# Reordering the blocks of a state-space scan, preparing a table's parts inside the loop before, and joining two matmuls of a feed-forward into a wide one

## The chip, the cores and the metric

The kernel runs on one core of a Trainium2 chip. The metric is the device time of one execution in microseconds (us). Five engines work side by side, each through its own instructions in order: TensorE (PE, with its weight loads as PEld), VectorE (DVE), ScalarE (ACT), GpSimd (POOL) and SyncE (SP), which issues the DMAs from HBM. The profile names them by these short forms.

## What is computed

Two model blocks over 256 tokens of width 1024, all in float32. The parts that the change touches are these, cut from the reference:

```python
# block 1: complex-diagonal state-space scan (32 groups of 16 channels, 64 states)
bu_re = jnp.einsum('blgc,gpc->blgp', uf, bbar_re)
bu_im = jnp.einsum('blgc,gpc->blgp', uf, bbar_im)
_, _, h_re, h_im = lax.associative_scan(_complex_scan_combine, (a_re, a_im, bu_re, bu_im), axis=1)
y = (jnp.einsum('blgp,gcp->blgc', h_re, c_re) - jnp.einsum('blgp,gcp->blgc', h_im, c_im)
     + d_skip * uf)
...
# block 1, end: retrieval of single-neuron experts, 16384 rows in each table
a = jnp.einsum('cd,ced->ce', xb, u_tab[eb])
w = gb * jax.nn.gelu(a, approximate=False)
out = jnp.einsum('ce,ced->cd', w, v_tab[eb])
...
# block 2, two layers, after the attention of each
h = _rms_norm(x, mlp_norm[l])
x = x + jnp.square(jax.nn.relu(h @ w_ff1[l])) @ w_ff2[l]     # 1024 -> 4096 -> 1024
```

Around them stand a window attention with its gates and branches in block 1, and compressed, selected and latent attention in block 2.

## The kernel before

The program is written in a tile framework. The code gives every instruction a priority that mostly follows the order in which it is written; at build time the framework fixes each engine's order from these priorities and the dependences. On the chip each engine goes through that order and waits at an instruction whose operands are not there yet.

**Weights.** A `Stream` loads weight pieces of 128 x 1024 float32 (512 KB) in one order through 3 raw buffers. For most products it splits a piece into a high part `whi` (cast by ACT, L120) and a remainder `wlo` (subtraction on DVE or POOL, L122), in two halves of 512 columns, through 3 buffers each. A product is then three matmuls: high times high, high times low, low times high.

**The scan.** `s5_scan` runs eight blocks of two groups each, in the background of other products: a generator whose steps are taken two at a time between the weight pieces of the query/key/value projection (L238, 24 matmuls of 512 columns on unsplit weights) and of the gates (L218, 128 of 256 columns). A block first makes a cosine and a sine table on DVE and POOL (L673 to L678) and its inputs by four matmuls (L683) into PSUM tiles `sc`; then rotates the inputs by the tables on DVE (L692 to L696), scans along the first 128 tokens (L703), carries over (L709 to L714), scans the second 128 (L717), rotates back (L720 to L723), and multiplies by the output matrix on PE (L730, eight matmuls). Each of these is one step, block after block. PE's order is thus projection matmuls with the scan's own matmuls among them. The attention scores of block 1 (L842, and L847 on DVE) use the same two banks `sc` as L683.

**The expert tables.** `peer` goes through the first table in 128 pieces. The step of a piece is 24 matmuls of 256 columns (L205 to L207); the activations (L986, L987, L989) land in `store`, one column of tokens per piece. Once the retrieval's choices are decoded, `quad` multiplies `store` by the routing weights, four tokens at a time, 64 times, spread over the pieces up to number `LAST` = 126 (L971, L972 on PE, L976 on DVE, L978 on ACT). Then the pool of that part is closed and the pool `pv` opened; `split` makes the parts `wh` and `wl` of a column of `store` (L1016 on ACT, L1017 on DVE), two columns ahead, and `gemm_acc` multiplies them with the second table's 128 pieces, 12 matmuls of 512 columns each (L273 to L275).

**The feed-forward.** `mlp` takes the first matrix in 32 pieces by `gemm_t`: for each of 8 contraction steps, three matmuls of 256 columns into one PSUM tile (L205 to L207). `evict` takes relu and the row scale on DVE (L1548), the square on ACT (L1549), the high part on ACT (L1550) and the remainder on DVE (L1551). The low parts of the weights alternate between DVE and POOL (`F1`). Three PSUM banks rotate. The second matrix follows with `gemm_acc` (12 matmuls of 512 columns per piece, 32 pieces).

Of the kernel before, what the change touches and what calls it, by code (L numbers as in the profile page):

```python
# [7 lines left out]
F32 = mybir.dt.float32  # L8
# [17 lines left out]
LAST = 126  # L26
# [170 lines left out]

class Kernel:
# [94 lines left out]
    def tokens(self):  # L293

        return [self.stay.tile([128, 8, T], F32R, name=n, tag=n) for n in ("xh", "xl")]

# [29 lines left out]
    def transposed_parts(self, src, i, xh, xl, tp, rev=None):  # L326

        n = src.shape[-1] // 128
        for k0 in range(0, n, 4):
# [9 lines left out]
            self.split_t(ps[:, :m], xh[:, k0:k0 + m, ts], xl and xl[:, k0:k0 + m, ts])  # L339
# [319 lines left out]
    def s5_scan(self, w, p, uT):  # L659
# [5 lines left out]
        for x in range(8):  # L665
            t, j0, n0 = x // 2, 2 * (x % 2), 2 * (x % 4)
            js = slice(2 * x, 2 * x + 2)
# [16 lines left out]
            yield  # L684
            tabs = [x.rearrange("p j a b -> p j (a b)") for x in (tc, ts)]
            cb, sb = [x.unsqueeze(2).to_broadcast([128, 2, 2, 128]) for x in tabs]
# [8 lines left out]
            yield  # L695
# [9 lines left out]
            yield  # L705
# [13 lines left out]
            yield  # L719
# [4 lines left out]
            yield  # L724
            if j0 == 0:
                yps = self.tp.tile([128, T], F32, name="tp", tag="tp")
            for i, (c, z) in enumerate(((self.cre, q2), (self.cre, q1), (self.cim, q3), (self.cn, im))):
                for j in range(2):
                    r = 32 * (j0 + j)
                    te.matmul(yps[r:r + 32].rearrange("p (u t) -> p u t", u=2), c[:, 2 * x + j], z[:, j],  # L730
                              start=i == 0, stop=i == 3)
            if j0:
                v.scalar_tensor_tensor(uT[:, t], uT[:, t], dsk[:, t:t + 1], yps, op0=OP.mult, op1=OP.add)
            yield
# [160 lines left out]
    def peer(self):  # L895
# [4 lines left out]
        with ExitStack() as outer:  # L900
# [4 lines left out]
            off = [0]  # L905

# [12 lines left out]
            with ExitStack() as ctx:  # L919
# [72 lines left out]
                def step():  # L992
# [7 lines left out]
                    while done["q"] < min(want, T // 4):  # L1000
                        quad(done["q"])

                self.gemm_t(128, 8, xh, xl, evict, step=step)
                while done["q"] < T // 4:
                    quad(done["q"])

            with ExitStack() as ctx:
                w = ctx.enter_context(tc.tile_pool(name="pv", bufs=1))
                ps = self.acc4(5, 6, 7, 3)
                self.next_gain("attn_norm_0")  # L1010
                parts = {}

                def split(c):
                    wh = w.tile([128, T], F32R, name="wh", tag="wh", bufs=3)
                    wl = w.tile([128, T], F32R, name="wl", tag="wl", bufs=3)
                    s.copy(wh, store[:, c])  # L1016
                    v.tensor_tensor(out=wl, in0=store[:, c], in1=wh.bitcast(F32), op=OP.subtract)  # L1017
                    parts[c] = wh, wl
# [692 lines left out]
```

## Time and profile before

| | us |
|---|---|
| median of 3 runs (1743.00 to 1745.09) | 1744.74 |
| the profiled execution | 1741.02 |
| its span, first to last instruction | 1739.2 |
| scan, under the query/key/value projection (40 to 110) | 70.0 |
| scan and attention, under the gates (110 to 200) | 90.0 |
| second expert table, from 732.4 on | 349.6 |
| first feed-forward matrix, layer 0 and layer 1 | 93.1, 93.2 |

The span is where the argument is made; the remainder of the profiled execution, 1.8 us, lies around it. A matmul's record lasts longer than the distance to the next start, since matmuls are pipelined; the pace is read from starts. A row of the timeline names the engine, line, operation and tiles; in square brackets stands how long the engine was idle before it and which instruction ended that. float32 matmuls on unsplit operands (L218, L238, L683, L730) have two records each.

### The profile page before, as it was taken

What the parts mean: (1) busy time and instruction counts of PE and PEld (TensorE: products, weight loads), DVE (VectorE), ACT (ScalarE), POOL (GpSimd) and SP (SyncE); (2) the same over time, 40 slices, a digit from 0 to 9 for tenths busy, and PEclk for the clock granted to TensorE, in tenths of its full rate; (3) what the DMA queues carried; (4) which work ended last, traced back from release to release, by engine and by line L of the source; (5) the groups of instructions that cost most, each with busy time, mean ns of one, the idle gap of its engine ahead of it and who ended that gap; (6) DMA issues with size and microseconds to landing.
All of it is one profiled execution on the core that took longest, in us unless ns stands there. A gap on an engine that the chain in (4) does not pass through costs nothing.

```text
span 1739.2 us, 30119 instructions
## 1 busy us (share of the span) xinstructions
PE 1679.5 (97%) x10796; PEld 1467.5 (84%) x10796; DVE 1066.5 (61%) x2590; ACT 871.6 (50%) x2054; POOL 600.0 (34%) x502
## 2 busy tenths in 40 slices
PE   7989998999999999999999999899999999999998
PEld 4467987999999999988888887787998878789986
DVE  5877344469878888755555555677653256775422
ACT  2014444454555554455555555655665455656643
POOL 1210365555000000044444444412544443144443
PEclk9999998899999999999999999999999999999999
DMA  6332445454655555556566665533555653335554
GB/s 224 109 96 73 135 144 160 135 187 138 183 160 158 162 161 164 170 177 193 193 193 193 193 194 183 173 103 122 172 189 187 194 180 123 134 132 189 181 192 143
DMA packets 81537, 282.34 MB, mean 162 GB/s; under 512 B 9659, under 2 KB 12524, under 8 KB 81388
## 3 DMA queue, kind: packets, MB, share of 16 engines
q1 hardware_dynamic: 81388, 280.43, 50.5%
q8 instruction: 85, 1.39, 0.3%
q14 instruction: 64, 0.52, 0.1%
HBM read 279.32 MB, written 1.07 MB: 161 GB/s over the span
## 4 chain that ended last, share of the span: by engine, by line
PE 82%; DVE 8%; POOL 4%; ACT 2%; issue 2%; DMA 2%; SPq 0%; POOLq 0%; DVEq 0%; ACTq 0%
PE acc L205 11%; PE acc L206 11%; PE acc L207 11%; PE acc L275 10%; PE acc L273 10%; PE acc L274 10%; PE acc L218 3%; POOL wlo L122 2%; PE o L1427 2%; PE acc L243 1%; PE acc L242 1%; PE acc L241 1%; ACT whi L120 1%; PE sc L1390 1%; PE g L971 1%
## 5 line engine op out<-in xcount | busy, mean ns | idle before, releaser
L122 POOL TENSOR_TENSOR wlo<-raw,whi 128x512 fp32r<-128x512 f32 (+2 forms) x396 | 518.8, 1323 | 947.8 <-ACT whi L120 903.6
L120 ACT CAST whi<-raw 128x512 fp32r<-128x512 f32 (+2 forms) x940 | 545.0, 613 | 402.1 <-PE acc L206 173.2
L122 DVE TENSOR_TENSOR wlo<-raw,whi 128x512 fp32r<-128x512 f32 (+2 forms) x544 | 412.0, 772 | 268.2 <-ACT whi L120 257.8
L205 PE MATMUL acc<-xh,whi 128*128 128x256 f32 x1664 | 477.9, 288 | 0.7 <-ACT xh L321 0.7
L207 PE MATMUL acc<-xh,wlo 128*128 128x256 f32 x1664 | 472.6, 284 | 1.6 <-DVE wlo L122 1.6
L206 PE MATMUL acc<-xl,whi 128*128 128x256 f32 x1664 | 472.6, 284 | 0.1
L207 PEld LDWEIGHTS acc<-xh,wlo 128*128 128x128 f32 x1664 | 320.4, 193 | 2.5 <-DVE wlo L122 1.8
L205 PEld LDWEIGHTS acc<-xh,whi 128*128 128x128 f32 x1664 | 320.3, 193 | 2.4 <-ACT xh L321 1.4
L206 PEld LDWEIGHTS acc<-xl,whi 128*128 128x128 f32 x1664 | 320.6, 193 | 1.4 <-issue 0.4
L273 PE MATMUL acc<-whi,wh 128*128 128x512 f32 x512 | 200.0, 391 | 2.8 <-ACT wh L1016 2.8
L274 PE MATMUL acc<-wlo,wh 128*128 128x512 f32 x512 | 199.8, 390 | 0.0
L275 PE MATMUL acc<-whi,wl 128*128 128x512 f32 x512 | 199.5, 390 | 0.0
L1016 ACT CAST wh<-store 128x256 fp32r<-128x256 f32 x128 | 52.0, 408 | 161.1 <-PE acc L274 160.2
L1017 DVE TENSOR_TENSOR wl<-store,wh 128x256 fp32r<-128x256 f32 x128 | 54.2, 425 | 115.3 <-ACT wh L1016 115.3
L273 PEld LDWEIGHTS acc<-whi,wh 128*128 128x128 f32 x512 | 96.5, 189 | 23.1 <-ACT wh L1016 3.0
L274 PEld LDWEIGHTS acc<-wlo,wh 128*128 128x128 f32 x512 | 96.6, 189 | 19.9
L275 PEld LDWEIGHTS acc<-whi,wl 128*128 128x128 f32 x512 | 96.4, 188 | 19.8
L274 PE MATMUL acc<-wlo,fh 128*128 128x512 f32 x256 | 99.7, 389 | 0.0
L275 PE MATMUL acc<-whi,fl 128*128 128x512 f32 x256 | 99.7, 389 | 0.0
L273 PE MATMUL acc<-whi,fh 128*128 128x512 f32 x256 | 99.6, 389 | 0.0
L218 PE MATMUL acc<-xt,raw 128*128 128x256 f32 x320 | 76.8, 389 | 0.0
L218 PEld LDWEIGHTS acc<-xt,raw 128*128 128x128 f32 x320 | 59.6, 193 | 12.5 <-issue 3.9
(384 smaller groups left out, 2443.7 us busy)
## 6 DMA issues: line engine op xcount, KB each, us to landing
raw<-in_peer_u_dram SPq DMA_DIRECT2D x128, 512.0 KB, 3.6
raw<-in_peer_v_dram SPq DMA_DIRECT2D x128, 512.0 KB, 4.3
raw<-in_w_ff_dram SPq DMA_DIRECT2D x128, 512.0 KB, 3.9
raw<-in_w_out_dram SPq DMA_DIRECT2D x24, 512.0 KB, 3.7
raw<-in_w_in_g_dram SPq DMA_DIRECT2D x16, 512.0 KB, 3.6
raw<-in_w_in_qkv_dram SPq DMA_DIRECT2D x12, 512.0 KB, 3.6
raw<-in_w_attn_branch_dram SPq DMA_DIRECT2D x8, 512.0 KB, 3.9
raw<-in_peer_w_query_dram SPq DMA_DIRECT2D x8, 512.0 KB, 3.9
```

Source lines behind the costliest of these rows:

```text
L120: nc.scalar.copy(hi[:, x], src[:, x])
L122: eng.tensor_tensor(out=lo[:, x], in0=src[:, x], in1=hi[:, x].bitcast(F32), op=OP.subtract)
L205: t.matmul(ps, wh, xh, start=first, stop=False)
L206: t.matmul(ps, wh, xl, start=False, stop=False)
L207: t.matmul(ps, wl, xh, start=False, stop=last)
L218: self.nc.tensor.matmul(ps, wh[:, k, m], xh[:, k], start=k == 0, stop=k == kt - 1)
L273: t.matmul(ps[i][n], xh[:, ts], w[0][:, ns], start=first, stop=False)
L274: t.matmul(ps[i][n], xh[:, ts], w[1][:, ns], start=False, stop=False)
L275: t.matmul(ps[i][n], xl[:, ts], w[0][:, ns], start=False, stop=last)
L1016: s.copy(wh, store[:, c])
L1017: v.tensor_tensor(out=wl, in0=store[:, c], in1=wh.bitcast(F32), op=OP.subtract)
L1427: te.matmul(o[:, 4 * b + x], st[u][:, c, x], val, start=c == 0, stop=c == i)
```

## The change

It has three parts. In `s5_scan` the steps become functions, and their order is new: the inputs of block x+1 (its tables and its four matmuls) stand ahead of the back-rotation of block x, and the outputs of block x stand behind the first rotation of block x+1. In `peer`, `LAST` is 124; the buffers of `wh` and `wl` lie in the outer pool; and columns 0 and 1 of `store` are split inside the first table's loop as soon as all 64 quads are done. In `mlp`, the high and low part of the tokens lie side by side in a tile, the matmuls high-high and high-low become one of 512 columns, and `evict` adds the two halves of the result, by a copy on ACT and an addition on DVE.

```diff
-LAST = 126
+LAST = 124
...
+class Halves:
+    def __init__(self, x, n):
+        self.x, self.n = x, n
+    def __getitem__(self, key):
+        p, ks, *ts = key
+        return self.x[ks.start // 4][(p, slice(0, 4), self.n, *ts)]
...
+    def tokens(self, both=False):
+        if both:
+            x = [self.stay.tile([128, 4, 2, T], F32R, name=n, tag=n) for n in ("xh", "xl")]
+            return x, [Halves(x, n) for n in range(2)]
...
+    def gemm_2(self, n_sub, x, evict):
+        t = self.nc.tensor
+        for s in range(n_sub):
+            wh, wl = [z.rearrange("p (k c) -> p k c", c=128) for z in self.S.get()]
+            ps = self.acc.tile([128, 2, T], F32, name="acc", tag="acc")
+            for k in range(8):
+                z = x[k // 4][:, k % 4]
+                if k:
+                    t.matmul(ps[:, 0], wl[:, k], z[:, 0], start=False, stop=False)
+                t.matmul(ps, wh[:, k], z, start=k == 0, stop=k == 7)
+                if k == 0:
+                    t.matmul(ps[:, 0], wl[:, k], z[:, 0], start=False, stop=False)
+            evict(s, ps)
...
-        for x in range(8):
...
+        inputs(0)
+        yield
+        for x in range(9):
+            if x < 8:
+                rotate(x)
+                yield
+            if x:
+                outputs(x - 1)
+                yield
+            if x < 8:
+                for f in (scan_1, scan_2):
+                    f(x)
+                    yield
+                if x < 7:
+                    inputs(x + 1)
+                    yield
+                back(x)
+                yield
...
+            def split(c):
+                wh = pst.tile([128, T], F32R, name="wh", tag="wh", bufs=3)
+                wl = pst.tile([128, T], F32R, name="wl", tag="wl", bufs=3)
...
+                    if done["q"] == T // 4 and c < 128 and 0 not in parts:
+                        split(0)
+                        split(1)
                 self.gemm_t(128, 8, xh, xl, evict, step=step)
-                while done["q"] < T // 4:
-                    quad(done["q"])
...
-                    if c == 0:
-                        split(0)
-                        split(1)
...
-                xh, xl = self.tokens()
+                x, (xh, xl) = self.tokens(True)
...
-                    v.scalar_tensor_tensor(r, ps, 0.0, row, op0=OP.max, op1=OP.mult)
+                    s.copy(r, ps[:, 1])
+                    v.tensor_tensor(out=r, in0=ps[:, 0], in1=r, op=OP.add)
+                    v.scalar_tensor_tensor(r, r, 0.0, row, op0=OP.max, op1=OP.mult)
                     s.activation(q, r, AF.Square)
...
-                self.gemm_t(32, 8, xh, xl, evict)
+                self.gemm_2(32, x, evict)
```

Three places show what this does to the engines' orders. The lines of the kernel after differ: L249 and L229 there are L238 and L218 before, L718 is L683, L783 is L730.

PE under the query/key/value projection, from the inputs of one scan block on (L683, L718: inputs; L730, L783: outputs), before:

```order
L683 MATMUL sc<-uT,bb 128x256 x4
L238 MATMUL acc<-raw,xt 128x512 x9
L730 MATMUL tp<-s5x,s5c 32x256 x6
L730 MATMUL tp<-bu,cn 32x256 x2
L238 MATMUL acc<-raw,xt 128x512 x3
L683 MATMUL sc<-uT,bb 128x256 x4
L238 MATMUL acc<-raw,xt 128x512 x11
```

and after:

```order
L718 MATMUL sc<-uT,bb 128x256 x4
L249 MATMUL acc<-raw,xt 128x512 x8
L718 MATMUL sc<-uT,bb 128x256 x4
L249 MATMUL acc<-raw,xt 128x512 x4
L783 MATMUL tp<-s5x,s5c 32x256 x6
L783 MATMUL tp<-bu,cn 32x256 x2
L249 MATMUL acc<-raw,xt 128x512 x8
L718 MATMUL sc<-uT,bb 128x256 x4
```

The inputs of the second block now stand ahead of the outputs of the first, and twelve projection matmuls lie between one block's outputs and the next block's.

ACT at the end of the first expert table (L986, L1065: activation of a piece; L978, L1057: a quad's copy; L1016, L982: high part of a `store` column), before:

```order
L978 ACTIVATE store<-g 128x2x4
L120 CAST whi<-raw 128x512
L986 ACTIVATE gt<-acc 128x256
L120 CAST whi<-raw 128x512 x2
L986 ACTIVATE gt<-acc 128x256
L120 CAST whi<-raw 128x512
L1016 CAST wh<-store 128x256 x4
```

and after:

```order
L1057 ACTIVATE store<-g 128x4x4
L982 CAST wh<-store 128x256 x3
L120 CAST whi<-raw 128x512
L1065 ACTIVATE gt<-acc 128x256
L120 CAST whi<-raw 128x512 x2
L1065 ACTIVATE gt<-acc 128x256
```

The first three `wh` now stand ahead of the activations of the last four pieces; before, they stood behind the last one.

DVE in the first feed-forward matrix, away from its ends (L1548, L1617: relu and scale; L1551, L1620: remainder of the square; L1616: the new addition), before:

```order
L1548 SCALAR_TENSOR_TENSOR fr<-acc,row 128x256
L122 TENSOR_TENSOR wlo<-raw,whi 128x512 x2
L1551 TENSOR_TENSOR fl<-fq,fh 128x256
L1548 SCALAR_TENSOR_TENSOR fr<-acc,row 128x256
L1551 TENSOR_TENSOR fl<-fq,fh 128x256
```

and after:

```order
L1616 TENSOR_TENSOR fr<-acc,fr 128x256
L1617 SCALAR_TENSOR_TENSOR fr<-fr,row 128x256
L122 TENSOR_TENSOR wlo<-raw,whi 128x512 x2
L1620 TENSOR_TENSOR fl<-fq,fh 128x256
L1616 TENSOR_TENSOR fr<-acc,fr 128x256
L1617 SCALAR_TENSOR_TENSOR fr<-fr,row 128x256
L1620 TENSOR_TENSOR fl<-fq,fh 128x256
```

The order is the old one with the addition put ahead of each scale. ACT's order there, after (L1615 is the new copy, L1618 the square, L1619 its high part):

```order
L120 CAST whi<-raw 128x512 x2
L1618 ACTIVATE fq<-fr 128x256
L1619 CAST fh<-fq 128x256
L1615 COPY fr<-acc 128x256
L120 CAST whi<-raw 128x512 x2
```

The copy of a piece stands behind the high part of the piece before, and the next weights' two casts lie between copy and square.

## Rows read from the trace of the kernel before

**Rows 1.** The page: an engine's busy time; a DMA's size and time to landing.

```profile
PE 1679.5 (97%) x10796; PEld 1467.5 (84%) x10796; DVE 1066.5 (61%) x2590; ACT 871.6 (50%) x2054; POOL 600.0 (34%) x502
...
raw<-in_peer_v_dram SPq DMA_DIRECT2D x128, 512.0 KB, 4.3
```

**Rows 2.** Stretches: length, busy PE, PEld, DVE, ACT, POOL, granted clock, DMA share, GB/s.

```profile
40.00:110.00 70.00, 63.17 (x247) 31.07 (x245) 61.68 (x162) 9.33 (x20) 16.53 (x10) 1.00 0.35 107
110.00:200.00 90.00, 89.56 (x554) 71.29 (x551) 53.75 (x181) 33.86 (x100) 8.23 (x7) 1.00 0.26 84
...
732.00:739.00 7.00, 4.25 (x16) 3.33 (x15) 2.97 (x5) 2.43 (x6) 1.79 (x2) 0.76 0.64 207
...
1229.00:1322.10 93.10, 93.10 (x777) 92.89 (x776) 51.43 (x101) 60.47 (x131) 45.94 (x35) 1.00 0.58 187
```

**Rows 3.** Waits between 30 and 205: us in total, times, longest.

```profile
DVE s5x L692 <- PE sc L683: 13.2, 4, 5.3
...
PE tp L730 <- DVE s5x L720: 6.7, 5, 3.2
```

**Rows 4.** Timeline of PE in the scan: start, us, what, [idle before <-releaser].

```profile
81.90 7.13 PE L238 MATMUL acc<-raw,xt 128*128 128x512 f32 x16
...
108.44 1.49 PE L730 MATMUL tp<-s5x,s5c 128*32 128x256 f32 x12 [3.15 <-DVE s5x L720]
```

**Rows 5.** Timeline of all engines where the second expert table begins.

```profile
730.95 0.42 DVE L987 TENSOR_TENSOR store<-gt,store 128x256 f32<-128x256 f32 x1
...
732.32 0.28 PE L207 MATMUL acc<-xh,wlo 128*128 128x256 f32 x1
...
733.31 1.27 POOL L122 TENSOR_TENSOR wlo<-raw,whi 128x512 fp32r<-128x512 f32 x1 [0.79 <-ACT whi L120]
...
733.50 1.36 DVE L987 TENSOR_TENSOR store<-gt,store 128x256 f32<-128x256 f32 x1 [2.13 <-ACT gt L986]
...
734.89 1.02 ACT L1016 CAST wh<-store 128x256 fp32r<-128x256 f32 x3 [0.92 <-DVE store L987]
...
735.35 0.80 PE L273 MATMUL acc<-whi,wh 128*128 128x512 f32 x1 [2.75 <-ACT wh L1016]
...
738.47 0.39 PE L274 MATMUL acc<-wlo,wh 128*128 128x512 f32 x1
```

**Rows 6.** Timeline of PE: starts of narrow, first wide and steady wide matmuls.

```profile
1240.02 0.28 PE L205 MATMUL acc<-xh,whi 128*128 128x256 f32 x1
...
1240.38 0.28 PE L205 MATMUL acc<-xh,whi 128*128 128x256 f32 x1
...
1322.10 0.40 PE L273 MATMUL acc<-whi,fh 128*128 128x512 f32 x1
1322.33 0.40 PE L274 MATMUL acc<-wlo,fh 128*128 128x512 f32 x1
1322.57 0.39 PE L275 MATMUL acc<-whi,fl 128*128 128x512 f32 x1
...
1330.06 0.39 PE L275 MATMUL acc<-whi,fl 128*128 128x512 f32 x1
...
1330.74 0.39 PE L275 MATMUL acc<-whi,fl 128*128 128x512 f32 x1
```

**Rows 7.** Groups by line and form, 1235 to 1320: count, busy us, mean ns, idle before.

```profile
L122 POOL TENSOR_TENSOR wlo<-raw,whi 128x512 fp32r<-128x512 f32 x30 | 41.6, 1406 | 42.7 <-ACT whi L120 42.7
L120 ACT CAST whi<-raw 128x512 fp32r<-128x512 f32 x62 | 35.5, 619 | 26.6 <-PE acc L206 25.1 <-DMA raw<-in_w_ff_dram 1.2
L122 DVE TENSOR_TENSOR wlo<-raw,whi 128x512 fp32r<-128x512 f32 x30 | 20.6, 725 | 2.4 <-ACT whi L120 1.3
L1551 DVE TENSOR_TENSOR fl<-fq,fh 128x256 fp32r<-128x256 f32 x30 | 13.8, 461 | 18.7 <-ACT fh L1550 18.7
L1548 DVE SCALAR_TENSOR_TENSOR fr<-acc,row 128x256 f32<-128x256 f32 x31 | 13.2, 425 | 18.5 <-PE acc L207 18.5
L1549 ACT ACTIVATE fq<-fr 128x256 f32<-128x256 f32 x30 | 12.5, 415 | 1.8 <-DVE fr L1548 1.8
```

More of the change, by code (lines that the diff above doesn't have):

```diff
@@ L338, in transposed_parts @@
             ts = slice(128 * i, 128 * i + 128)
-            self.split_t(ps[:, :m], xh[:, k0:k0 + m, ts], xl and xl[:, k0:k0 + m, ts])
+            part = lambda x: x[:, k0:k0 + m, ts]
+            self.split_t(ps[:, :m], part(xh), xl and part(xl))
     def rstd(self, i, out=None):
@@ L663, in s5_scan, with place, inputs @@
         ec, es = self.ec, self.es
-        for x in range(8):
-            t, j0, n0 = x // 2, 2 * (x % 2), 2 * (x % 4)
-            js = slice(2 * x, 2 * x + 2)
+        st = [{} for _ in range(8)]
+        out = {}
+        def place(x):
+            return x // 2, 2 * (x % 2), slice(2 * x, 2 * x + 2)
+        def inputs(x):
+            t, j0, js = place(x)
             tc, ts = [w.tile([128, 2, 8, 16], F32, name=n, tag=n, bufs=2) for n in ("tabc", "tabs")]
@@ L694, in s5_scan, with scan_1 @@
             v.tensor_tensor(out=q1, in0=q1, in1=q4, op=OP.subtract)
-            yield
+            st[x].update(q1=q1, q2=q2, q3=q3, q4=q4, cb=cb, sb=sb)
+        def scan_1(x):
+            t, j0, js = place(x)
+            q1, q2, q3 = st[x]["q1"], st[x]["q2"], st[x]["q3"]
             v.tensor_tensor(out=q3, in0=q3, in1=q2, op=OP.add)
@@ L704, in s5_scan, with scan_2 @@
                                          op0=OP.mult, op1=OP.add)
-            yield
+            st[x].update(re=re, im=im, mg=mg)
+        def scan_2(x):
+            t, j0, js = place(x)
+            q1, q3, re, im, mg = st[x]["q1"], st[x]["q3"], st[x]["re"], st[x]["im"], st[x]["mg"]
             ini = w.tile([128, 6, 2], F32, name="ini", tag="ini", bufs=2)
@@ L718, in s5_scan, with back @@
                                          initial=ini[:, c, j:j + 1], op0=OP.mult, op1=OP.add)
-            yield
+        def back(x):
+            t, j0, js = place(x)
+            q1, q2, q3, re, im, cb, sb = st[x]["q1"], st[x]["q2"], st[x]["q3"], st[x]["re"], st[x]["im"], st[x]["cb"], st[x]["sb"]
             v.tensor_tensor(out=q2, in0=im, in1=sb, op=OP.mult)
@@ L723, in s5_scan, with outputs @@
             v.tensor_tensor(out=im, in0=im, in1=cb, op=OP.mult)
-            yield
+        def outputs(x):
+            t, j0, js = place(x)
+            q1, q2, q3, im = st[x]["q1"], st[x]["q2"], st[x]["q3"], st[x]["im"]
             if j0 == 0:
-                yps = self.tp.tile([128, T], F32, name="tp", tag="tp")
+                out[0] = self.tp.tile([128, T], F32, name="tp", tag="tp")
             for i, (c, z) in enumerate(((self.cre, q2), (self.cre, q1), (self.cim, q3), (self.cn, im))):
@@ L905, in peer @@
             off = [0]
+            parts = {}
+            def split(c):
+                wh = pst.tile([128, T], F32R, name="wh", tag="wh", bufs=3)
+                wl = pst.tile([128, T], F32R, name="wl", tag="wl", bufs=3)
+                s.copy(wh, store[:, c])
+                v.tensor_tensor(out=wl, in0=store[:, c], in1=wh.bitcast(F32), op=OP.subtract)
+                parts[c] = wh, wl
             def scratch(shape, dt=F32):
```

23 lines of the change are left out of this document (8 added, 15 removed).

## The prediction

> **What bounds the kernel now.** I read the page first: PE is busy in 97% of the span, the others in two thirds at most [rows 1]. So what counts is where PE stands still, and how fast it goes where it doesn't. The stretches show three places that the change touches [rows 2]. From 40 to 110 PE is busy 63.17 of 70.0 us: 6.8 us of standing, and the waits name it: PE's output matmuls of the scan wait for DVE's back-rotation, 6.7 us in 5 waits, the longest 3.15 [rows 3, 4]. DVE in turn waits 13.2 us for the scan's inputs from PE [rows 3]: the two take turns, since a block's inputs stand on PE behind the outputs of the block before. From 732 to 739 PE is busy 4.25 of 7.0 us, at a mean granted clock of 0.76. And in the first feed-forward matrix PE never stands (93.10 of 93.10 us): there only a shorter PE program helps, as long as nobody else becomes the slowest.
>
> **The scan's new order.** It removes no instruction and adds none; it moves them. Between the outputs of one block and of the next, PE now has twelve projection matmuls and the inputs of the next block. Sixteen records, eight matmuls, take 7.13 us [rows 4], so twelve take 10.7 us. In that time DVE must do one block's rotation, scans and back-rotation. Over the 70 us of about five blocks DVE was busy 61.68 us, 12.3 per block with everything else, and PE 63.17, 12.6 per block [rows 2]. PE is thus slightly the longer one, and DVE can stay ahead once its own 13.2 us of waiting for inputs are gone. That is tight: the floor of the stretch is 63.2 us, so the gain is 6.8 at most; if DVE keeps as many gaps as before it is nothing. What comes late next I take from the order: where the attention scores begin, the second score matmuls need the banks that DVE empties, and DVE has the second scan and two back-rotations of a block ahead of that, where PE stood only 0.4 us in 90 before [rows 2]. I put 1.7 us there, an estimate about halfway between 0 and the longest wait of the stretch before, 3.15 [rows 4]. Taken: 6.7 - 1.7 = 5.0 us, ends 0 and 6.8. POOL's one table product per block moves ahead with the inputs; POOL is busy 16.5 of 70 us there, which covers it.
>
> **The parts of the second table.** PE's last narrow matmul starts at 732.32; at the 0.120 us pace (below) the next could start at 732.44. It starts at 735.35, since the activation of the last piece (DVE until 734.86), then the cast of column 0, come first [rows 5]. That is 2.91 us. Then seven wide matmuls take until 738.47, 3.12 us, where the steady pace of 0.227 gives 1.59: 1.53 us lost at the half clock after the standing. After the change the first three casts stand ahead of the last four pieces' activations, at least three pieces, 3 x 24 x 0.120 = 8.6 us, before they are needed, and only column 127 depends on the last activation. So 2.91 + 1.53 = 4.4 us go. The work moved is three casts and three subtractions, hidden under pieces on which PE is the slowest; the 64 quads are packed into two pieces fewer out of more than eighty, and what they put on PE stays the same. On SP the load of the next norm's gain moves ahead of two raw loads and must wait until the last quad has read the buffer that it overwrites. Behind it stands the load of the second table's piece 1. Three raw buffers are three pieces of 12 x 0.227 = 2.7 us, 8.2 in all, against 4.3 us to landing [rows 1], so up to 3.9 us of delay cost nothing. Without that cover the same wait would come back, so the ends are 1.5 and 4.4; I take 4.4.
>
> **The wide feed-forward.** Narrow matmuls start every 0.120 us (0.36 for three), wide ones every 0.227 (0.68 for three) [rows 6]. A step of the contraction costs 3 x 0.120 = 0.360 before and 0.120 + 0.2267 = 0.3467 after: 0.0133 less. There are 8 x 32 x 2 = 512 steps: 6.8 us. The row that is nearest to a mixed stream is the start of the second matrix, where the first two wide ones after narrow ones lie 0.23 and 0.24 apart [rows 6]; with 0.235 a step saves 0.005, in all 2.6 us. I take the steady pace, from rows with hundreds of matmuls, and 2.6 as the low end. The Trainium skill speaks against this part: "TensorE: Matmul & The Clock Gate", section "Back-to-back issue gap", gives a matmul its columns plus a fixed 2.5 ns. By that, one matmul fewer per step would give 512 x 2.5 ns = 1.3 us. This case's trace disagrees: two narrow ones cost 13 ns more than a wide one of as many columns.
>
> Added are a copy on ACT and an addition on DVE for each of 64 pieces. The nearest rows are 0.415 us (L1549) and 0.425 (L1548) [rows 7], so 13.3 and 13.6 us per layer. ACT was busy 60.47 and DVE 51.43 of 93.1 us there [rows 2]; 73.8 and 65.0 still fit under PE's 89.7. In order, though, each piece makes a loop: DVE's addition and scale, ACT's square and cast, DVE's remainder, then the next piece's addition. With POOL taking the low weights: 0.425 + 0.425 + 0.415 + 0.415 + 0.461 = 2.14 us. With DVE taking them, two subtractions of 0.725 cover the ACT steps: 0.425 + 0.425 + 1.45 + 0.461 = 2.76 [rows 7]. A pair is 4.90, PE's pair 16 x 0.3467 = 5.55. It fits, with three banks to level the two. At the start a wide matmul needs both parts of both token halves, one subtraction later than before: 0 to 0.73 us per layer by the nearest row (L122 on DVE); I take 0.4, 0.8 for both. The part gives 6.8 - 0.8 = 6.0 us, ends 1.1 and 6.8.
>
> **The sum.** 5.0 + 4.4 + 6.0 = 15.4 us off the profiled execution: 1741.0 to 1725.6. The median of the runs is 3.7 us above that execution; the same difference on the median gives 1744.7 - 15.4 = 1729.3.
>
> **The rivals.**
> 1. *The wide matmuls save little.* If a wide one after a narrow one keeps the 0.235 of its first starts, the part is worth 1.8 instead of 6.0, and the kernel takes 1733.5. For it speak three starts, against it hundreds. The Trainium skill's rule above lands on this side.
> 2. *DVE sets the scan's pace.* It has 61.7 of PE's 63.2 us to do, in order, with the query work between. If the waits only move, the scan gives nothing: 1734.3.
> 3. *The table's start still waits*, for a weight piece behind the gain's load or for a bank: the change does not do what it says there, 1744.7 - 11.0 = 1733.7. The order of ACT speaks against it.
> 4. *Better: the narrow pace was the loads'.* PEld is busy 92.89 of 93.10 us in that stretch [rows 2], and a third of its loads go. If a narrow matmul beside a wide one takes half of the wide one's time, 0.1133, a step saves 0.020, 10.2 us in place of 6.8: 1725.9, and with the whole 6.7 of the scan 1724.2. Against it: no row shows a narrow one at that pace.
> 5. *Slower: the evict loop becomes the clock of the first feed-forward matrix.* The scale had one operand in PSUM; now both lie in SBUF, beside POOL's subtraction. A DVE product of that kind took 1.36 us instead of 0.42 while POOL worked, 0.94 more [rows 5]. Two such holds in a pair make 4.90 + 1.88 = 6.78 us where 5.76 stood: 32 pairs lose 33 us, and with the 9.4 of the other parts the kernel takes 1744.7 + 33 - 9.4 = 1768. It eats the whole gain from 5.76 - 4.90 + 9.4/32 = 1.15 us of holds per pair on. Against it: the remainder (L1551) has both operands in SBUF already, with POOL at work 41.6 of 85 us, and its mean is 0.461, only 0.036 above the scale's [rows 7]. The Trainium skill says the same of the danger: "SBUF — State Buffer", section "Who interferes with whom", has a DVE instruction with two SBUF inputs contend with a GpSimd one that reads SBUF, the first holding the other up for its whole length. By that rule the scale is newly exposed; the two rows show both what a hold costs and how seldom it falls there.
>
> **How the numbers follow.** Chances: the forecast 0.48; rival 1 0.15; rival 2 0.13; rival 3 0.05; two of these three together (about 1738) 0.05; rival 4 0.08; rival 5 0.06. The likeliest is the forecast, 1729.3. The range takes in the upper end of the parts (6.8 + 4.4 + 10.2 = 21.4 off, 1723.3) and two failed parts together (15.4 - 4.2 - 5.0 = 6.2 off, 1738.5), and leaves out rival 5 and what lies beyond: 1723.5 to 1738.5. A measurement of this kernel can tell about 0.2% from no change, 3.5 us. Every case but rival 5 is past that on the fast side, unless all three parts fail: faster 0.90, same 0.04, slower 0.06.
>
> **What would show it.** In the profile after, PE's waits for back-rotations in the scan should be near zero and its busy time from 40 to about 103 full, with a new wait of 1 to 2 us at the scores. The first matmul of the second table should start 0.1 to 0.2 us behind the last of the first, at full clock. In the first feed-forward matrix a wide and a narrow start together should span 0.347 us, a piece 2.77, the stretch 90 us without a PE gap, with the scale's mean below 0.6. Wrong I would be if PE stood in the feed-forward, waiting for a bank, or if the time from the scan's start to the gates' end were not 4 to 7 us shorter.

## The result and the profile after

The changed kernel takes 1722.6 us (median of four runs, 1718.6 to 1732.9) against 1744.9 before: a ratio of 0.9876, 95% interval 0.9852 to 0.9901. It is faster, as forecast, but by 22 us where 15.4 were forecast (1729.3), and the median lies 0.9 us below the range's low end. Five more runs, e9_after below, gave a median of 1724.7 and a ratio of 0.9886 (0.9862 to 0.9910). Two of the other 40 runs of the kernel before took 4978 and 7685 us and are left out everywhere below. The profiled execution is the slowest of the nine, 1732.94 us, so its own length says little; its stages say what happened. The page's head:

```profile
span 1731.2 us, 29130 instructions
...
PE 1680.2 (97%) x10284; PEld 1447.7 (84%) x10284; DVE 1117.5 (65%) x2654; ACT 887.8 (51%) x2116; POOL 597.9 (35%) x502
```

PE is as busy as before [rows 1], with 512 matmuls fewer; DVE has 64 instructions more. Starts of matmuls in the two traces, in us. "Half clock" is a granted clock of 0.5, the 1.2 GHz level; elsewhere it is 1.0, 2.4 GHz.

| place | before | after | difference of lengths |
|---|---|---|---|
| first projection matmul of the scan's stretch | 33.61 | 34.50 | |
| last gates matmul | 195.21 | 185.78 | 161.61 to 151.28: -10.3 |
| last matmul of the first table | 732.32 | 722.58 | |
| first matmul of the second table | 735.35 | 722.70 | 3.03 to 0.12: -2.9, and the half clock behind it: -1.5 |
| first feed-forward matrix, layer 0 | 1229.07 to 1322.10 | 1220.31 to 1310.86 | 93.03 to 90.56: -2.5 |
| the same, layer 1 | 1551.59 to 1644.62 | 1546.02 to 1636.58 | 93.03 to 90.56: -2.5 |
| half-clock time in the span | 28.0 in 4 stretches | 45.6 in 7 | this execution: +17.5 at half clock, some 8.8 lost where PE sets the pace |

The stretches that answer to [rows 2] (length, busy PE, PEld, DVE, ACT, POOL, granted clock, DMA share, GB/s):

```profile
40.00:110.00 70.00, 70.00 (x290) 37.68 (x289) 68.74 (x184) 10.67 (x23) 14.78 (x11) 1.00 0.39 119
110.00:185.80 75.80, 75.56 (x471) 60.65 (x470) 46.12 (x159) 31.17 (x95) 3.41 (x3) 1.00 0.27 84
722.00:729.00 7.00, 7.00 (x36) 5.92 (x35) 3.53 (x5) 3.72 (x9) 3.32 (x3) 1.00 0.59 194
1220.30:1310.70 90.40, 90.40 (x519) 78.43 (x518) 72.89 (x130) 67.28 (x159) 43.59 (x33) 1.00 0.56 186
```

From 40 to 110 PE stood 6.8 us before and no longer stands; 290 matmul records lie there where 247 did. From 110 to the last gates matmul it stands 0.24 us. At the table's start PE is busy all 7 us at full clock, 36 records in place of 16. In the feed-forward PEld, which was busy throughout, now has 12 us free, and DVE goes from 51 to 73.

The timeline of PE in the scan (start, us, what), beside [rows 4]:

```profile
46.15 1.13 PE L718 MATMUL sc<-uT,bb 32*128 32x256 f32 x8
47.21 3.70 PE L249 MATMUL acc<-raw,xt 128*128 128x512 f32 x8
50.84 1.49 PE L783 MATMUL tp<-s5x,s5c 128*32 128x256 f32 x12
52.16 0.60 PE L783 MATMUL tp<-bu,cn 128*32 128x256 f32 x4
52.69 7.13 PE L249 MATMUL acc<-raw,xt 128*128 128x512 f32 x16
59.76 1.13 PE L718 MATMUL sc<-uT,bb 32*128 32x256 f32 x8
```

Inputs of the next block, four projections, a block's outputs in one piece, eight projections, and again. No line carries an idle time, where a line of L730 before carried 3.15 us. From start to start, each of the eight passages from a projection or gates matmul to an output takes 0.52 or 0.31 us, with no wait in it (e8 below has the old order's).

All engines where the second table begins, beside [rows 5]:

```profile
722.58 0.28 PE L218 MATMUL acc<-xh,wlo 128*128 128x256 f32 x1
...
722.70 0.40 PE L284 MATMUL acc<-whi,wh 128*128 128x512 f32 x1
...
722.93 0.40 PE L285 MATMUL acc<-wlo,wh 128*128 128x512 f32 x1
...
723.72 1.39 DVE L1066 TENSOR_TENSOR store<-gt,store 128x256 f32<-128x256 f32 x1 [2.14 <-ACT gt L1065]
```

The last activation of the first table is still held on DVE, 1.39 us beside POOL, and ends at 725.1, but nothing waits for it any more: the second table is 2.4 us under way, at 0.23 us a matmul.

The groups of the first feed-forward matrix by form, 1224 to 1300 (count, busy us, mean ns, idle before), beside [rows 7]:

```profile
L122 POOL TENSOR_TENSOR wlo<-raw,whi 128x512 fp32r<-128x512 f32 x27 | 37.2, 1398 | 39.9 <-ACT whi L120 39.9
...
L1617 DVE SCALAR_TENSOR_TENSOR fr<-fr,row 128x256 f32<-128x256 f32 x27 | 25.6, 950 | 0.9
...
L1620 DVE TENSOR_TENSOR fl<-fq,fh 128x256 fp32r<-128x256 f32 x26 | 12.0, 462 | 11.4 <-ACT fh L1619 11.4
L1616 DVE TENSOR_TENSOR fr<-acc,fr 128x256 f32<-128x256 f32 x27 | 11.2, 414 | 2.9 <-ACT fr L1615 2.9
```

The scale, 425 ns before, has a mean of 950: the hold by POOL that rival 5 named is there. And PE, which runs through, pays nothing for it (e4 below).

### The profile page after: what moved, and what is told of

Same layout as the page of the kernel before. It is cut to its first block, busy times and chain, and to the rows that moved or that the text cites. A ratio compares the mean times of both kernels' runs of the same rounds, so it can differ in the third digit from the quotient of the medians.

```text
span 1731.2 us, 29130 instructions
## 1 busy us (share of the span) xinstructions
PE 1680.2 (97%) x10284; PEld 1447.7 (84%) x10284; DVE 1117.5 (65%) x2654; ACT 887.8 (51%) x2116; POOL 597.9 (35%) x502
## 4 chain that ended last, share of the span: by engine, by line
PE 83%; DVE 7%; POOL 3%; ACT 2%; issue 2%; DMA 2%; SPq 0%; POOLq 0%; DVEq 0%; ACTq 0%
PE acc L286 10%; PE acc L284 10%; PE acc L285 10%; PE acc L216 7%; PE acc L321 7%; PE acc L218 7%; PE acc L217 7%; PE acc L229 4%; PE acc L320 3%; PE acc L249 2%; PE o L1494 2%; POOL wlo L122 2%; PE acc L253 1%; PE acc L252 1%; PE acc L254 1%
## 5 line engine op out<-in xcount | busy, mean ns | idle before, releaser
L216 PE MATMUL acc<-xh,whi 128*128 128x256 f32 x1152 | 333.3, 290 | 0.7 <-ACT xh L350 0.7
L218 PE MATMUL acc<-xh,wlo 128*128 128x256 f32 x1152 | 327.5, 284 | 2.0 <-DVE wlo L122 2.0
L217 PE MATMUL acc<-xl,whi 128*128 128x256 f32 x1152 | 328.0, 285 | 0.1
L218 PEld LDWEIGHTS acc<-xh,wlo 128*128 128x128 f32 x1152 | 221.5, 192 | 3.0 <-DVE wlo L122 2.4
L216 PEld LDWEIGHTS acc<-xh,whi 128*128 128x128 f32 x1152 | 221.5, 193 | 1.9 <-ACT xh L350 1.1
L217 PEld LDWEIGHTS acc<-xl,whi 128*128 128x128 f32 x1152 | 221.7, 192 | 1.4 <-issue 0.4
L982 ACT CAST wh<-store 128x256 fp32r<-128x256 f32 x128 | 51.9, 407 | 158.1 <-PE acc L285 158.1
L321 PE MATMUL acc<-xh,whi 128*128 128x512 f32 x256 | 95.4, 396 | 0.0
L321 PE MATMUL acc<-xl,whi 128*128 128x512 f32 x256 | 92.2, 396 | 0.0
```

The source lines that it names most:

```text
L216: t.matmul(ps, wh, xh, start=first, stop=False)
L217: t.matmul(ps, wh, xl, start=False, stop=False)
L218: t.matmul(ps, wl, xh, start=False, stop=last)
L321: t.matmul(ps, wh[:, k], z, start=k == 0, stop=k == 7)
```

## The experiments

**Each part alone, on the kernel before.** The edits are the three parts of the diff above, one at a time: the scan's generator (e1), `LAST = 124` with the two early splits and their pool (e2), `gemm_2` with its tokens and `evict` (e3).

> The kernel before with the scan's new order alone. Theory A (the trace after, read from start to start of the matmuls): the new order takes 9 to 10 us off the stretch from the scan's first matmuls to the last gates matmul, 8 of it from PE's waits for the back-rotations and up to 2 from fewer changes between the scan's 32- and 64-row matmuls and the projections' 128-row ones; the kernel takes about 1735.5. Rival B (the forecast's size): 5.0 us, 1740, and the rest of the gain measured comes from how the half-clock stretches fell. Rival C (DVE sets the pace): no more than 1 us. The two other parts' places stay as they were: 2.9 us of standing before the second table, 93.0 us for each first feed-forward matrix. Half-clock stretches of 3.4 to 10.2 us fall differently from run to run and move the whole time by a few us; the stretches' lengths, less half of the half-clock time in them, decide.

1731.4 us (1729.2 to 1733.4), ratio 0.9929 (0.9912 to 0.9946). The stretch from the first projection to the last gates matmul is 151.29 us where it was 161.61, 10.3 less, as in the whole change. The profiled execution has half-clock stretches of the same lengths as the profiled one before (10.24, 10.24, 3.41 and, at the end, 4.2 and 4.1 us), and so the two can be compared as they are: 1741.02 to 1731.14, 9.9 less. Theory A holds, and the forecast's 5.0 is half of it.

```profile
40.00:110.00 70.00, 70.00 (x291) 37.99 (x290) 68.74 (x185) 10.98 (x23) 14.77 (x11) 1.00 0.36 115
```

> The kernel before with the early parts of the second table alone (the quads end two pieces sooner, the first two columns are cast and split ahead of the last pieces' activations). Both theories: PE goes from the first table's last matmul to the second table's first in under 0.25 us (3.03 before) and at full clock, 4.4 us less from the last first-table matmul to the eighth second-table one; the kernel takes 1740.5. Rival: the quads packed closer cost PE or DVE time in the first table; then the stretch of the first table is longer by what the kernel lacks of the 4.4.

1740.4 us (1737.3 to 1743.9), ratio 0.9981 (0.9969 to 0.9992): 4.0 less. PE's timeline at the seam, 0.12 us from the last narrow to the first wide start and no half clock:

```profile
734.93 0.28 PE L207 MATMUL acc<-xh,wlo 128*128 128x256 f32 x1
735.05 0.40 PE L273 MATMUL acc<-whi,wh 128*128 128x512 f32 x1
735.29 0.40 PE L274 MATMUL acc<-wlo,wh 128*128 128x512 f32 x1
```

The first table itself is not longer, 449.28 us from its first matmul to its last where it was 449.46. The part does what the forecast said, in the size that it said.

> The kernel before with the wide first feed-forward matrix alone. Theory A (the trace after): a matrix takes 90.56 us in place of 93.03, two of them 4.9 less; the kernel takes 1740, and the pieces alternate between 2.77 and 2.82 us, since DVE's scale is held by POOL in one of two pieces. Rival B (the forecast's size): 6.0 us, 1739. Rival C: the hold grows without the other parts, the pair of pieces comes to 5.76 us or more and nothing is gained, 1745.

1738.5 us (1736.1 to 1744.3), ratio 0.9972 (0.9957 to 0.9986): 5.9 less by the medians. The two matrices give less, 93.03 to 90.63 us each from the first matmul to the second matrix's first, 4.8 in all, and that doesn't depend on where half-clock time fell. The pieces that I had read as alternating 2.77 and 2.82 us are, counted from the right matmul, 2.795 and 2.798: the expectation's second half was an artefact of mine.

The three medians add up to 22.9 us, the whole change gave 22.3 and, in e9, 19.0. The parts do not help or hinder each other within what half-clock time blurs.

**Is the evict loop the clock of the feed-forward?**

```diff
-                    v.tensor_tensor(out=r, in0=ps[:, 0], in1=r, op=OP.add)
-                    v.scalar_tensor_tensor(r, r, 0.0, row, op0=OP.max, op1=OP.mult)
+                    v.tensor_tensor(out=ps[:, 0], in0=ps[:, 0], in1=r, op=OP.add)
+                    v.scalar_tensor_tensor(r, ps[:, 0], 0.0, row, op0=OP.max, op1=OP.mult)
```

> The changed kernel with one edit: the addition of the two halves is written back to PSUM and the scale reads it there, so that the scale has one operand in SBUF where it had two. Theory A (POOL holds the scale, and the evict loop sets the pace of every second piece): the scale's mean falls from 932 to about 430 ns, every piece takes 2.772 us, a matrix 88.8 to 89.8 us in place of 90.56, the kernel 1.6 us less than the changed one. Rival B (the pieces of 2.82 have another reason, the weight parts or a bank): the scale falls, the pieces keep 2.77 and 2.82, the time doesn't move. Rival C (the addition with two operands in SBUF and PSUM is held in its place): its mean rises above 0.8 us and nothing is gained.

```profile
L1620 DVE TENSOR_TENSOR fl<-fq,fh 128x256 fp32r<-128x256 f32 x29 | 26.0, 897 | 13.2 <-ACT fh L1619 13.2
...
L1617 DVE SCALAR_TENSOR_TENSOR fr<-acc,row 128x256 f32<-128x256 f32 x27 | 11.5, 424 | 0.9
```

Groups of the same kind as above, in 1224 to 1300 of this kernel. The scale is free of POOL, 424 ns, but the remainder (L1620), the next DVE instruction with both operands in SBUF, is held in its place, 897 ns in place of 462. The matrix is 90.41 us to its last matmul, 90.33 in the changed kernel; the kernel took 1725.7 (1721.4 to 1727.4). Rival B: the hold moves, and PE's pace does not depend on where it falls. The loop is not far from setting the pace, though. In the changed kernel no copy but a matrix's first waits for PE, and the copies (ACT, L1615) advance by 5.62 us for every two pieces, where PE needs 5.59. First come two copies of the changed kernel, twenty pieces apart, then one of e4:

```profile
1251.58 0.37 ACT L1615 COPY fr<-acc 128x256 f32<-128x256 f32 x1
...
1307.77 0.37 ACT L1615 COPY fr<-acc 128x256 f32<-128x256 f32 x1
```

```profile
1304.83 0.37 ACT L1615 COPY fr<-acc 128x256 f32<-128x256 f32 x1 [0.46 <-PE acc L321]
```

So the loop falls behind PE by 0.03 us a pair, and over a matrix's sixteen pairs the three banks take that up. In e4 the pair takes 5.45 us, and the loop catches up until the copies wait for PE. Whether a longer matrix would come to wait for the changed kernel's loop was not tried.

**Which half of the scan's order does it?**

```diff
 e5: outputs right behind the back-rotation
-            if x:
-                outputs(x - 1)
...
             back(x)
+            outputs(x)
 e6: inputs right ahead of the rotation
+                inputs(x)
                 rotate(x)
...
-                if x < 7:
-                    inputs(x + 1)
```

> The changed kernel with half of the scan's new order: the inputs of the next block stay ahead of the back-rotation, but a block's outputs stand right behind its back-rotation again. Measured by the stretch from the first projection matmul behind the scan's start to the last gates matmul: 163.5 us before, 153.2 with the whole order. Theory A (what counts is that PE doesn't come to the outputs before DVE has rotated back): PE still waits at the outputs, and the stretch is 158 to 162. Rival B (what counts is that DVE never waits for inputs): it is within 1 us of 153.2.

> The changed kernel with the other half of the scan's new order: a block's outputs stand behind the next block's rotation, but the inputs of that block come right ahead of its rotation, behind the back-rotation. Same stretch, 163.5 before and 153.2 with the whole order. Theory A: the outputs are never early, PE doesn't wait there, and the stretch is 153 to 156. Rival B: DVE waits for the inputs in every block, falls behind, and PE waits for it at the scores or at the gates: 158 to 162.

These two and e7 and e8 are one execution each; their stretches hold no half-clock time and are compared by length. Their expectations count the stretch from a place 1.9 us earlier: 163.5 there is 161.61 here, 153.2 is 151.28. Both stretches are 151.29 us, the changed kernel's to 0.01. The reason lies ahead of the chip: on PE, DVE, ACT, POOL and SP both kernels have the changed kernel's instructions in the changed kernel's order, but for buffer names. The program's order is only a priority there, and what either half alone brings about, and the old code doesn't, is that the inputs of a block come ahead of the outputs of the block before. These two runs therefore tell nothing apart between my theories; they say that this one inversion is the whole of the part.

**Who sets the pace of the scan, and how much of the gain was waiting?** The four products of the back-rotation are left out, of the changed kernel (e7) and of the kernel before (e8).

```diff
-            v.tensor_tensor(out=q2, in0=im, in1=sb, op=OP.mult)
-            v.tensor_tensor(out=q1, in0=re, in1=cb, op=OP.mult)
-            v.tensor_tensor(out=q3, in0=re, in1=sb, op=OP.mult)
-            v.tensor_tensor(out=im, in0=im, in1=cb, op=OP.mult)
```

> The changed kernel without the four products of the scan's back-rotation (the outputs read the scan's values unrotated), some 3 us of DVE less in each of eight blocks. It tells who sets the pace of the new order, where both engines' rows read as full. Theory A (PE does, its floor is reached): the stretch stays at 153.2, within 0.5 us. Rival B (DVE does): it is 2 to 10 us shorter. Rival C (half and half, where blocks are dense): about 1 us shorter.

```profile
40.00:110.00 70.00, 70.00 (x299) 38.91 (x298) 55.81 (x165) 11.59 (x24) 13.28 (x11) 1.00 0.36 113
```

The stretch is 150.94 us, 0.34 less, and that stands in the starts of the score matmuls (their pitches sum to 7.89 us where the changed kernel has 8.26). DVE, busy 68.74 of 70 us in the changed kernel, is busy 55.81 here, and from 40 to 110 PE goes no faster. So PE sets the pace of the new order: rival 2 is refuted, and 151 us is the floor for this order of matmuls.

> The kernel before without the four products of the scan's back-rotation. It splits the 10.3 us that the new order gives into waits and the rest. Theory A (8 us of PE's waits for the back-rotation, 2 us of matmul changes that stay): the waits go with the products, the changes stay, and the stretch is 155 to 156 in place of 163.5. Rival B (all is waiting): 153.2. Rival C (the waits are then for the scans themselves, which stand right ahead): 158 to 161.

The stretch is 152.85 us in place of 161.61: 8.8 of the 10.3 go with the products, in the old order. In the expectation's count that is 154.8, just below theory A's 155 to 156. From start to start the matmuls of the trace before say the same. Where PE passes undisturbed from a gates or projection matmul to an output matmul, it takes 0.31 or 0.52 us; seven of these twelve passages take longer, by 3.22, 1.52, 1.12, 0.71, 0.60, 0.48 and 0.04 us, in all 7.7. The other 2.6 us of the 10.3 are no waits for the back-rotation. Of them 2.0 stand in two sums over the same matmuls: the outputs' own pitch, 15.68 us before and 14.81 after, and the scores', 9.43 and 8.26. With them goes the number of changes into or out of 32-row matmuls (the scan's inputs and outputs), 45 before and 32 after; such a change costs, for one, 0.31 us from an output to a gates matmul, where two outputs start 0.10 apart on average. In e8 there are 34, and of the 1.6 us that it stays above the changed kernel 1.3 stand in the same two sums, 15.35 and 9.06. That the changes make up all of the 2.6 is argued, not shown; no run alters them alone.

**The base, and the matmuls' order in the feed-forward.** e9 is the changed kernel, unaltered; e10 and e13 change the order of a piece's sixteen matmuls.

```diff
 e10: wide, narrow, narrow, wide, wide, ...
-                if k:
+                if k % 2:
                     t.matmul(ps[:, 0], wl[:, k], z[:, 0], start=False, stop=False)
                 t.matmul(ps, wh[:, k], z, start=k == 0, stop=k == 7)
-                if k == 0:
+                if k % 2 == 0:
                     t.matmul(ps[:, 0], wl[:, k], z[:, 0], start=False, stop=False)
 e13: eight wide, then eight narrow
...
+            for k in range(8):
+                t.matmul(ps, wh[:, k], x[k // 4][:, k % 4], start=k == 0, stop=False)
+            for k in range(8):
+                t.matmul(ps[:, 0], wl[:, k], x[k // 4][:, k % 4, 0], start=False, stop=k == 7)
```

> The changed kernel once more, unaltered, as the base of the two runs beside it. Half-clock time differs from run to run, so its median over more runs is what the whole gain is measured by: by the sum of the three parts run alone (13.0 + 4.0 + 5.9 us off 1744.4) 1721.5, by the first four runs 1722.6.

1724.7 us (1721.4 to 1729.2). The nine runs of the changed kernel go with their mean granted clock, from 1718.6 at 0.993 and 1720.2 at 0.994 to 1732.9 at 0.987. Span times mean granted clock takes that out, as far as PE sets the pace throughout: 1708.4 (standard error 0.6) for these nine, 1724.5 (0.2) for the 38 runs of the kernel before made beside these experiments. By that measure the change is worth 16.2 us at full clock; the rest of its 19.5 us of mean difference is less half-clock time, a mean clock of 0.9917 in place of 0.9898, and 1.5 of it is the table's start. The stages of the traces give 18.1 us at full clock (10.3, 2.9 and 4.9). Why the two differ by 1.9 stays open.

> The changed kernel with the matmuls of the first feed-forward matrix in another order: wide, narrow, narrow, wide, wide, narrow, ... so that half of them follow one of their own width. The step is 0.3497 us now, where the steady paces of either width give 0.120 + 0.2267 = 0.3467. Theory A (a wide matmul behind a narrow one is what costs, 0.234 in place of 0.227): the wide ones behind a wide one start 0.227 after it, the step falls to 0.347 or 0.348, a matrix from 90.4 to about 89.8. Rival B (the cost is that of the mixed stream as such, its weight loads or operands, wherever the change falls): the step stays at 0.350 within 0.0005.

1721.3 us (1718.5 to 1722.0), ratio 0.9869 (0.9843 to 0.9895); that is not told apart from the changed kernel's. The matrix is: 90.07 us to its last matmul where e9 has 90.34 and 90.41, the piece 2.787 where it was 2.797. Single matmuls in PE's timeline:

```profile
1250.27 0.28 PE L323 MATMUL acc<-xl,wlo 128*128 128x256 f32 x1
1250.38 0.28 PE L320 MATMUL acc<-xl,wlo 128*128 128x256 f32 x1
1250.50 0.40 PE L321 MATMUL acc<-xl,whi 128*128 128x512 f32 x1
1250.74 0.40 PE L321 MATMUL acc<-xh,whi 128*128 128x512 f32 x1
1250.97 0.28 PE L323 MATMUL acc<-xh,wlo 128*128 128x256 f32 x1
```

The narrow ones take 0.11 and 0.12, the first wide one 0.24, and the wide one behind it 0.23, not the 0.227 of theory A. In between: 0.3484 a step.

> The changed kernel with the first feed-forward matrix fully sorted: a piece's eight wide matmuls first, then its eight narrow ones. Theory A (the cost sits at each change of width): with two changes a piece instead of sixteen the piece falls from 2.797 to 2.774 plus little, 2.775 to 2.780, where the order in pairs gave 2.787. Rival B (a wide matmul's 0.227 in the second matrix is another stream, with the weights and the tokens in other places): the wide ones behind wide ones keep 0.231 to 0.235, the piece stays at 2.785 or above.

```profile
1250.48 1.11 PE L318 MATMUL acc<-xh,whi 128*128 128x512 f32 x4
1251.42 1.08 PE L318 MATMUL acc<-xl,whi 128*128 128x512 f32 x4
1252.34 0.64 PE L320 MATMUL acc<-xh,wlo 128*128 128x256 f32 x4
1252.81 0.64 PE L320 MATMUL acc<-xl,wlo 128*128 128x256 f32 x4
1253.29 1.09 PE L318 MATMUL acc<-xh,whi 128*128 128x512 f32 x4
```

Fully sorted, four wide ones take 0.94 and 0.92 us, 0.23 each; narrow ones 0.47 and 0.48, 0.12 each; most pieces take 2.79 to 2.83, 2.80 on average, no better than in pairs. Theory A is out: the cost does not sit at the changes of width. In this stream a step takes 0.348 to 0.350 in any order, and the 0.2267 of the second matrix's wide matmuls isn't reached. What makes the two streams differ stays open. (The kernel as a whole takes 1728.5 us, ratio 0.9912, 0.9892 to 0.9932: a whole first matrix takes 92.3 us to the second's first matmul, 1.7 more than in e9, PE standing 1.2 us in it for the tokens' low parts and 0.5 in the seventh piece for a bank, and the second matrix is 0.9 us longer; I didn't follow that up.)

**The same widening where the slack is smaller.** The first table and its query matrix get `gemm_2` too, with the copy and the addition ahead of the activation.

```diff
+                    gs = w.tile([128, T], F32, name="gs", tag="gs", bufs=2)
+                    s.copy(gs, ps[:, 1])
+                    v.tensor_tensor(out=ps[:, 0], in0=ps[:, 0], in1=gs, op=OP.add)
+                    ps = ps[:, 0]
...
-                self.gemm_t(128, 8, xh, xl, evict, step=step)
+                self.gemm_2(128, x2, evict, step=step)
...
-PU = 'v'
+PU = 'vg'     (e11 only: low parts shared with POOL)
```

> The changed kernel with the same widening in the first table and its query matrix: 136 pieces of 8 steps, so 1088 steps, with a copy on ACT and an addition on DVE for each piece, and the low parts of the table's weights shared by DVE and POOL in place of DVE alone. Theory A (a step saves the 0.0103 us measured in the feed-forward, and the engines have room): 11 us less, 1711. Rival B (DVE, busy 235 of 282 us there and with 37 more to do, or POOL's holds on it, becomes the pace): nothing gained or slower than the changed kernel, 1722 to 1740.

1764.2 us (1753.5 to 1768.8), ratio 1.0114 (1.0084 to 1.0143), slower than both kernels. The table's last matmul starts at 756.55, in e9 at 722.30. The stretch 420 to 740, then rows of DVE's and POOL's groups from 500 to 740, PE's wait there, and DVE's timeline:

```profile
420.00:740.00 320.00, 299.52 (x1919) 250.29 (x1918) 313.52 (x542) 169.56 (x495) 137.78 (x89) 0.99 0.41 145
```

```profile
L122 POOL TENSOR_TENSOR wlo<-raw,whi 128x512 fp32r<-128x512 f32 x66 | 98.5, 1493 | 142.3 <-DVE spare L1042 73.3 <-ACT whi L120 31.8 <-ACT gt L1076 28.0
...
L1077 DVE TENSOR_TENSOR store<-gt,store 128x48 f32<-128x48 f32 (+32 forms) x66 | 72.9, 1105 | 0.5
```

```profile
PE acc L321 <- ACT store L1079: 14.7, 32, 0.8
```

```profile
600.36 1.36 DVE L1077 TENSOR_TENSOR store<-gt,store 128x132 f32<-128x132 f32 x1
...
604.29 0.28 DVE L1077 TENSOR_TENSOR store<-gt,store 128x132 f32<-128x132 f32 x1
```

The same product on the same 132 columns takes 0.28 us or 1.36. Its mean is 1.1 us, 0.8 more than with POOL idle (below), DVE is busy 314 of 320 us, and PE waits for banks 32 times, 14.7 us in all. This is rival 5 of the prediction, at another place.

> The widened first table once more, with the low parts of the table's weights all on DVE, as they are in the changed kernel, so that POOL stands still there in the table's second half. The version that shared them took 1764, and DVE's product of the table's activations rose from 0.31 to 1.1 us. Theory A (POOL's holds are what cost): the product is back at 0.31 to 0.35 us, DVE does 235 us and 37 more in some 272 and just keeps up, the table is 5 to 11 us shorter than in the changed kernel and the whole takes 1714 to 1719. Rival B (DVE's own work is too much, with its order): the product is back, but PE waits for banks, and the whole takes 1724 to 1740.

1727.8 us (1727.0 to 1732.9), ratio 0.9912 (0.9888 to 0.9935). The stretch 420 to 722, and the product's group from 480 to 720:

```profile
420.00:722.00 302.00, 299.08 (x2002) 257.31 (x2001) 292.46 (x660) 187.33 (x527) 8.93 (x4) 0.99 0.50 165
```

```profile
L1077 DVE TENSOR_TENSOR store<-gt,store 128x256 f32<-128x256 f32 (+36 forms) x75 | 24.1, 321 | 0.9 <-ACT gt L1076 0.2
```

With POOL still, the product is back at 321 ns, and 36 us of the 40 are back: the holds were the cost. But DVE is busy 292 of 302 us, PE is no longer full, and the clock falls three times for 3.4 us in the table (at 367, 394 and 439). The table's last matmul starts at 720.56, 1.7 us ahead of e9's, where 5 to 11 were hoped for. Between the two theories: the holds explain e11, and the version doesn't beat the changed kernel. That DVE's own work takes the rest fits its busy time but was not tried.

## Why the prediction was too slow, step by step

**What bounds the kernel** held: PE, and the three places. **The table** held in mechanism and size: 4.4 us forecast, 2.9 of standing and 1.5 of half clock gone in the trace, 4.0 measured alone. Its cover held too: PE is busy 7.00 of 7.00 us from 722 on, at full clock.

**The scan** failed in size, 10.3 where 5.0 were taken; the prediction's own sign, a stretch not 4 to 7 us shorter, says so. It failed through three steps. "The floor of the stretch is 63.2 us, so the gain is 6.8 at most" took busy time for need. First, the 6.7 us of waits of [rows 3] are idle time between records; a matmul's record goes on past the point at which the next could start (0.39 us at a pitch of 0.23), so each wait hides its first part. From start to start it is 7.7, and 1.0 was missing. Second, busy time also holds the longer pitches around changes of matmul shape; the new order has thirteen such changes fewer and 2.6 us less of pitch, a term that the sum didn't have. Third, of the wait of 1.7 at the scores, halfway between 0 and 3.15, no more than 0.4 came: PE stands 0.24 us from 110 to the last gates matmul, and in e7 the scores' pitches are 0.37 shorter. The 2.6 is what is left after that wait, so 1.0 + 2.6 + 1.7 = 5.3. The argument for DVE keeping up (12.3 us a block against 12.6) was right, and narrower than it looked: DVE is busy 98% of the stretch, and e7 shows that it still isn't the pace.

**The wide feed-forward** was right in kind and 1.1 us too large: 4.9 for 6.0. A step takes 0.3497 us where 0.3467 were taken, so 512 steps give 5.3 and not 6.8; the two starts cost 0.4 and not 0.8. The step that failed is the 0.2267 of [rows 6], measured in a stream of wide matmuls only; the low row beside it, 0.235, is nearer to the 0.234 that came. Rival 1 with its 1.8 us was still too low, since the narrow ones became faster at the same time, 0.116 in place of 0.120, which is rival 4's direction in a small size. The Trainium skill ("TensorE: Matmul & The Clock Gate", section "Back-to-back issue gap") gives an isolated matmul a fixed 2.5 ns beside its columns, by which 512 steps would save an estimated 1.3 us; the trace shows 10.3 ns a step, four times that.

**Rival 5** came half: its hold is there, 950 ns in place of 425 for the scale, about 1.05 us in a pair of pieces, close to the 1.15 from which it was to eat the gain, and yet it costs nothing. What failed is the loop of 4.90 us a pair, which added in a row what the engines overlap: with the hold it should be 5.95, and it is 5.62, so little above PE's 5.59 that the banks cover it. e4 takes the hold off the scale and PE doesn't notice. "The scale's mean below 0.6" as a sign was therefore wrong, though the conclusion stood. e11 shows where the mechanism does decide: where DVE is already full.

**The sum.** Scan +5.3, table 0, wide -1.1: 15.4 becomes 19.6 us. The median of the first four runs lies 2.7 us further down, and half-clock time, which moves single runs by 14 us, covers that: nine runs have a median of 1724.7, 19.6 below the 1744.3 of before. That the two agree to the tenth is luck: of the second some 3.3 us are half-clock time (e9), of the first only the table's 1.5. The range's low end allowed all terms at their upper ends, 21.4; since 6.8 was no upper end for the scan, it stood too high.

## What to carry to other kernels

Measure waits of TensorE from start to start of the matmuls, not as idle time between records, and do not read busy time as a floor: it holds the longer pitches at changes of matmul shape, and a new order can save some of them. Where the code's order is only a priority, look at the order that comes out: two different rewritings here were the same program. A DVE instruction with both operands in SBUF beside POOL's work is safe only while its loop has slack or the banks can take up the lag; compare the loop's pace with PE's over a whole pair of pieces first, then widen.

## What the runs showed of the hardware

- A hold by POOL moves to the next exposed DVE instruction, one with both operands in SBUF. Freed at the scale (950 to 424 ns), it came at the remainder (462 to 897). In the table a product of 132 columns took 0.28 us, or 1.36 beside a subtraction on POOL. The Trainium skill's "SBUF — State Buffer", section "Who interferes with whom", names the shared port as an exclusive lock; both traces agree.
- Matmuls on split parts (fp32r), each with a weight load, start at a pace that depends on the stream: narrow 0.120 and wide 0.227 us in streams of their own kind, 0.116 and 0.234 in turns, 0.12 and 0.23 sorted within a piece. In the mixed stream the sum of the two hardly depends on the order, 0.348 to 0.350.
- From start to start, passing from a projection or gates matmul to one of the scan's 32-row ones takes 0.31 us behind 256 columns and 0.52 behind 512, in all passages of the changed kernel's scan and in those before that hold no wait.
- Half-clock stretches between 1090 and 1510 us, three or four of 3.4 to 10.2 us, stand in the profiled executions of the changed kernel (two) and of e8, one in e11 (13.7 us) and e12 (10.2), and none in the kernel before, e1 to e7, e10 and e13. In the same program (the changed kernel, and e5 and e6 with its order on every engine) they come and go between executions; what decides was not found.
